# Moving the pool with x and its split parts above the weight buffers and temporaries in SBUF

## The chip, the core and the metric

The kernel runs on one core of a Trainium2 chip. The metric is the device time in microseconds (us) of one execution. A profile of one execution, with the duration and the start of each instruction on each engine, is read beside the times. The engines are PE (the matrix engine; PEld are its weight loads), DVE (vector), ACT (scalar), POOL and SP; SP issues nearly all transfers here.

## The reference

The program is an encoder trunk of two layers over 256 tokens of width 1024, all in float32. A layer is a mixer and a convolutional feed-forward:

```python
for l in range(DEPTH):
    h = _rmsnorm(x, mix_norm[l])
    x = x + _mixer(h, w_in[l], ...)      # gated delta rule + HGRN2, both directions
    h = _rmsnorm(x, ffn_norm[l])
    x = x + _conv_ffn(h, w_up[l], ...)   # 1024 -> 2 x 2816, conv of 3, SiLU gate, -> 1024
return _rmsnorm(x, final_norm)
```

Nearly all of the arithmetic is in the matrix products with w_in, the two branch weights, w_out, w_up and w_down.

## The kernel before, in words

Activations stay in SBUF with channels on the partitions and tokens in the free direction. A product is made with both operands split in two float32r parts, high and low: the weight piece `raw` (128 x 1024) is loaded by SP, ACT copies it to `wh` (line 204), and DVE writes the rest, `wl = raw - wh` (line 205). There are three buffers each of `raw`, `wh` and `wl`, used in turn. Each product then takes three matmuls per 128 x 128 block of weights (lines 240 to 242):

```python
self.g.mm(o, whm, a)      # high weights, high activations
self.g.mm(o, whm, b)      # high weights, low activations
self.g.mm(o, wlm, a)
```

Each such matmul (line 146) loads 128 columns of weights (512 bytes of each partition) into PE and streams 256 columns of activations (1024 bytes of each partition) past them. The next weights are loaded while the present activations stream. The names of the streamed operands tell the stages apart. In the trace a name in front of the comma is the streamed operand, the one behind it the loaded one:

- `xh`, `xl`: the split input of a mixer or of the feed-forward. They are streamed 3 x 1152 times. In 3 x 160 further matmuls, whose output has tokens on the partitions, they are the loaded operand and `wh`, `wl` are streamed. Of the 3 x 1152, 2 x 22 x 48 = 2112 belong to the product with w_up.
- `ohl`: the normalized outputs of the two mixer branches, for the branch weights (`pbr`, lines 928 to 930): 384 matmuls.
- `mhi`, `mlo`: the merged branches, for w_out: 3 x 128 matmuls.
- `hh`, `hl`: the hidden activations of the feed-forward, for w_down: 3 x 352 matmuls.

`xh`, `mhi` and `hh` go through the same helper (class `Gemm`, line 208), with the same order of instructions; only the tiles differ. A few products (lists in `OPT["f32"]`) are made in plain float32 from `raw` and `xnt`, which the trace shows as two matmuls each.

SBUF is given out by tile pools, one above the other in the order in which they are opened: `cp` holds constants, `xp` holds x, x times the norm's weight (`xw`), sums of squares and the split parts `xh` and `xl`, `wp` the weight buffers, `tp` temporaries. The pools of a stage, with `ohl`, `mhi`, `hh` and the rest (`mp0`, `fp0`, `mp1`, `fp1`), are opened above these and closed again. The order of the instructions is set by a scheduler from priorities in the code and does not look at addresses.

Of the kernel before, what the change touches and what calls it, by code (L numbers as in the profile page):

```python
# [14 lines left out]
PSUM = bass.MemoryType.PSUM  # L15
DRAM = bass.MemoryType.DRAM

P = 128
T = 256
# [55 lines left out]

# columns of the per-layer vector pack (one value per partition each)
V_MIX = 0
# [9 lines left out]

# columns of the constants
C_ID = 0
# [27 lines left out]
def trunk(ctx: ExitStack, tc: tile.TileContext, x_in, consts, masks, vec, rows, w16, w_in, w_br, w_out, w_up, w_down, out):  # L117
    nc = tc.nc
    PRE = OPT["pre"]
# [3 lines left out]
    cp = ctx.enter_context(tc.tile_pool(name="cp", bufs=1))  # L123
    xp = ctx.enter_context(tc.tile_pool(name="xp", bufs=1))
    wp = ctx.enter_context(tc.tile_pool(name="wp", bufs=3))
    tp = ctx.enter_context(tc.tile_pool(name="tp", bufs=4))
    pg = ctx.enter_context(tc.tile_pool(name="pg", bufs=3, space=PSUM))
    pm = ctx.enter_context(tc.tile_pool(name="pm", bufs=5, space=PSUM))
# [10 lines left out]
    class Group:  # L139
        """Matmuls accumulating in one PSUM bank, kept in order; one start, one stop."""  # L140

# [3 lines left out]
        def mm(self, o, lhsT, rhs, after=None):  # L145
            self.prev = chain(pe.matmul(o, lhsT, rhs, start=self.i == 0, stop=self.i == self.n - 1), self.prev)  # L146
            chain(self.prev, after)
            self.i += 1

    # ---------------------------------------------------------------- constants  # L150
    epst = cp.tile([P, 1], F32, name="epst")
# [3 lines left out]
    x = []  # L155
# [9 lines left out]
    for item in OPT["x0"]:  # L165
        if item < 4:
            sp.dma_start(xt[item], x_in[item])
        else:
            s = slice(512 * (item - 4), 512 * (item - 3))
# [9 lines left out]
    lower = cst[:, C_L:C_L + P]  # L179
    ones = cp.tile([P, P], F32, name="ones")  # L180
    pool.memset(ones, 1.0)

    # ---------------------------------------------------------------- helpers
    def tmp(name, tag="tmp"):
        return tp.tile([P, 512], F32, tag=tag, name=name, bufs=OPT[tag])

    def piece(src, n):
        raw = wp.tile([P, 1024], F32, tag="raw", name="raw", bufs=OPT["raw"])
        sp.dma_start(raw[:, :n], src)
        return raw  # L190
# [17 lines left out]
    class Gemm:  # L208
        """src[i]: [P, k, 256] pieces; fills a bank: two column tiles (T layout) or two token tiles."""

# [38 lines left out]
    def gemm32(src, xw, tokens=False):  # L249
        """As gemm, with float32 operands as they are."""  # L250
        ps = pg.tile([P, 512], F32, tag="g", name="ps", bufs=OPT["g"])
        g = Group(KT * 2)
        for k0 in range(0, KT, 4):
            raw = piece(src(k0 // 4), 1024).rearrange("p (k c) -> p k c", c=256)
            for kk in range(4):
                a = xw[k0 + kk]
                for m in range(2):
                    o = ps[:, m * 256:(m + 1) * 256]
                    if tokens:
                        g.mm(o, a[:, m * P:(m + 1) * P], raw[:, kk, :])  # L260
                    else:
                        g.mm(o, raw[:, kk, m * P:(m + 1) * P], a)
        return ps
# [6 lines left out]
    class Rms:  # L270
        """1 / sqrt(mean of squares + eps) of the tokens: on all partitions (rb), and per token (rt)."""

# [38 lines left out]
    class SplitX:  # L311
        """x times the norm's weight, in two parts."""

# [15 lines left out]
    class Pre:  # L329
        """The first projections of a mixer (PRE), from x times the norm's weight."""  # L330

# [12 lines left out]
        def ahead(self, l):  # L344
            """Splits the weights of some more projections."""
            if not OPT["es"][l]:
                return
            self.stack = ExitStack()
            pool = self.stack.enter_context(tc.tile_pool(name=f"ep{l}", bufs=1, side="right", reuse_waits=OPT["rw"]))
            n = 2 * len(OPT["es"][l])  # L350
            with tc.high_priority(offset=OPT["eo"]):
                for c in OPT["es"][l]:
                    self.parts[c] = [split_piece_(w_in[l, c, i], 1024, pool, n) for i in range(2)]
# [5 lines left out]
        def mm(self, items, after=None):  # L359
            """Products of (projection, k), one after the other."""  # L360
            for j, k in items:
                w = self.raw[j][k // 4].rearrange("p (k c) -> p k c", c=256)
                for m in range(2):
                    self.g[j].mm(self.ps[j][:, m * 256:(m + 1) * 256], w[:, k % 4, m * P:(m + 1) * P], self.x[k],
                                 after or self.last)
                    after = None
                    self.last = self.g[j].prev
# [4 lines left out]
    def mixer(l, pre, rs):  # L372
        V = vecs[:, l]
        with ExitStack() as mc:
# [11 lines left out]
            def small(name, n=8):  # L386
                return mp.tile([P, 2, n], F32, name=name)
# [14 lines left out]

            # ---- 1 / rms; the first projections are scaled after the product, the others before
            xw = pre.x
# [8 lines left out]
            rbp, rt = rs  # L413
            rb = mp.tile([P, T], F32, name="rb")
# [16 lines left out]

            # ---- beta, decays and their sums, tokens on partitions
            beta, cs, nea = small("beta"), small("cs"), small("nea")
# [48 lines left out]

            # ---- projections, conv and silu of q, k, v: [channel, token]
            qk = mp.tile([P, 2, H, T], F32, tag="qk", name="qk")
# [32 lines left out]

            # ---- sums of squares of q and k; k and v with tokens on partitions
            ssk = mp.tile([P, 2, H], F32, name="ssk")
# [49 lines left out]

            # ---- decays: exp of the smaller difference serves both directions  # L570
            dfb = []
# [20 lines left out]

            # ---- Gram blocks: per direction and block the transposed system [0] and the attention weights [1]
            np_ = mp.tile([P, 2, 2, 8, P], F32, tag="np", name="np_")
# [9 lines left out]

            # ---- inverses of the diagonal 32 x 32 blocks, one system per partition, columns on two halves
            def solve():
# [40 lines left out]

            # ---- T: inverse, R: its transpose. Blocks of 32 to 64 to 128
            def inverse():
# [41 lines left out]

            # ---- delta rule: first chunk, state, second chunk, outputs
            osb = []
# [50 lines left out]

            # ---- gates
            sgs, sz = [], []
# [21 lines left out]

            # ---- HGRN2, two heads at a time
            hg = {}  # L770
# [32 lines left out]
            def hgrn(e):  # L803
                qr, kb, t0 = hg["q", e], hg["k", e], hg["f", e]
                qa = late().tile([P, 2, 512], F32, tag="qa", name="qa")
                t1 = late().tile([P, 2, 256], F32, tag="tt1", name="tt1")
                at = late().tile([P, 2, 2, T], F32, tag="at", name="at")
                # qa: [backward, forward]; kb, t0: [forward, backward]
                dve.tensor_tensor(qa[:, 0], qr, t0[:, 1], ALU.mult)
                dve.tensor_tensor(qa[:, 1], qr, t0[:, 0], ALU.mult)  # L810
                ks = tmp("ksum", "tmh")
                dve.tensor_tensor(ks, kb[:, 0], kb[:, 1], ALU.add)
                # the block pairs u = (head, block): diagonal blocks of the weights, [s, t]
                diag = view(at[:, 0, 0, 0:1], [[512, 2], [384, 2], [1, P]])
                offd = view(at[:, 0, 0, P:P + 1], [[512, 2], [128, 2], [1, P]])
                pa = bank("pa", (2, 2, P), "h")
                for u in range(4):
                    pe.matmul(pa[:, u // 2, u % 2], ks[:, u * P:(u + 1) * P], qr[:, u * P:(u + 1) * P],
                              start=True, stop=True)
                act.copy(diag, pa)  # L820
                tc_, tn = t0, t1
                for n, h in enumerate(LEVELS):
# [6 lines left out]
                    for u in range(4):  # L829
                        pe.matmul(pa[:, u // 2, u % 2], kc[:, u * P:(u + 1) * P],  # L830
                                  view(qa[:, 0, u * P:u * P + 1], [[2 * h, 64 // h], [512 + h, 2], [1, h]]),
                                  start=True, stop=True)
# [34 lines left out]
                ob = late().tile([P, 2, 2, P], F32, tag="ob", name="ob", bufs=OPT["obb"])  # L867
# [5 lines left out]
            def out_norm(kind, ob, b, h0, nh, cc, sz, w):  # L873
                """ob: [P tokens, nh, 128] of block b, normalized, gated, transposed and split."""
                if not hl:
# [15 lines left out]
                for h in range(nh):  # L891
                    on = tp.tile([P, P], F32, tag=("s128", "s12h")[kind], name="on", bufs=(5, 2)[kind])
# [16 lines left out]

            # ---- branches, merge, output projection  # L910
            mh, ml = [], []
# [130 lines left out]
    def meet(pre, rs, todo, n):  # L1042
        """The rest of the first projections, the sums of squares among them."""
        pre.mm(todo[:n])
        rm, rs = rs, rs.finish(pre.last if n else None)
        pre.mm(todo[n:], rm.last)
        return rs, rm

    first = [raw0]
# [9 lines left out]
    rs, rm = meet(pre, rs, todo[OPT["e0"]:], OPT["fa0"])  # L1059
    # lower bounds of the forget gates: softmax over the layers, cumulated, less the first  # L1060
    lbm = cp.tile([P, 8], F32, name="lbm")
# [29 lines left out]
    for l in range(OPT["layers"]):  # L1091
        nxt = mixer(l, pre, rs)
        pre, rs = ffn(l, *nxt)
    # ---- final norm: tokens on partitions
    op = ctx.enter_context(tc.tile_pool(name="op", bufs=4, reuse_waits="tile"))
# [11 lines left out]
    rt = rs.per_token(prev)  # L1107
    prev = rs.last
    turn(3)
    for i in range(4):  # L1110
        h, b = divmod(i, 2)
        o = op.tile([P, 4 * P], F32, tag="o", name="o")
        src = pts[i].rearrange("p k c -> p (k c)")
# [84 lines left out]
```

## Time and profile before

| What | Value |
|---|---|
| time, median of three runs | 928.67 us (927.70 to 929.71) |
| span of the profiled execution, first to last instruction | 926.8 us |
| PE busy | 906.6 us, 98% |
| DVE busy | 668.5 us, 72% |
| ACT busy | 559.0 us, 60% |
| split float32r matmuls on PE | 3456 + 480 with x, 384 with ohl, 384 with mhi and mlo, 1056 with hh and hl |

The profile gives the profiled execution's own time as its span alone; the median lies 1.9 us above it, which is what lies around the span. Matmuls are pipelined: the duration of one (285 ns, say) is longer than the distance from its start to the next start, and only that distance, the pitch here, adds up to time. It is read where the chain of work that ended last is an unbroken run of matmuls: the length of the run divided by their number.

### The profile page before, as it was taken

The page shows a single profiled execution, that of the slowest core. Times are in us where ns is not written, and L with a number is a line of the kernel's source. Part 1 is how long each engine was busy: PE and PEld are TensorE (multiplying, and loading weights), DVE is VectorE, ACT ScalarE, POOL GpSimd, SP SyncE. Part 2 cuts the span into 40 slices and gives each one's busy share as a digit, 9 for nine tenths or more (in the row PEclk, how much of TensorE's full clock was granted, in tenths as well). Part 3 has the DMA queues.
Part 4 walks back from the last instruction along what each step waited for, and adds up shares of the span by engine and source line. Part 5 has one row for each costly group of instructions (what it writes and reads, how often), then busy time and mean ns, then how long its engine had stood idle before and what let it go on. Part 6 is the DMA issues. An engine that isn't in the chain of part 4 may idle for free.

```text
span 926.8 us, 18732 instructions
## 1 busy us (share of the span) xinstructions
PE 906.6 (98%) x7450; PEld 887.8 (96%) x7450; DVE 668.5 (72%) x1279; ACT 559.0 (60%) x974; POOL 13.9 (2%) x123
## 2 busy tenths in 40 slices
PE   7999999999999999999999999999999999999997
PEld 6988999999999999999989899999999999999996
DVE  4667997655877888865447889885667788888543
ACT  4698647678566555543437856665855665555443
POOL 0000000000000000000000000000000000000000
PEclk9999999999999999999999999999999999999999
DMA  6455554225567655555505564533265656555552
GB/s 207 137 189 169 171 184 124 69 74 177 183 202 250 186 183 183 183 176 174 171 27 170 183 205 149 152 100 92 91 197 175 192 184 187 183 183 183 171 183 80
DMA packets 51111, 150.07 MB, mean 162 GB/s; under 512 B 13488, under 2 KB 14032, under 8 KB 50768
## 3 DMA queue, kind: packets, MB, share of 16 engines
q1 hardware_dynamic: 50304, 147.96, 50.5%
q8 instruction: 58, 0.95, 0.4%
q10 hardware_dynamic: 720, 0.92, 0.3%
q14 instruction: 29, 0.24, 0.1%
HBM read 146.75 MB, written 2.11 MB: 161 GB/s over the span
## 4 chain that ended last, share of the span: by engine, by line
PE 88%; ACT 4%; DMA 3%; DVE 3%; issue 1%; SPq 0%; DVEq 0%; ACTq 0%
PE ps L146 72%; PE pbr L146 5%; PE pa L830 3%; DMA raw<-in_w_in_dram 2%; DVE wl L205 1%; DMA ld<-dg 1%; PE po L146 1%; PE poh L146 1%; PE psb L146 1%; ACT wh L204 1%; PE ss L146 0%; PE pz L666 0%; PE pr L689 0%; DMA xs<-in_consts_dram 0%; DVE pr L627 0%
## 5 line engine op out<-in xcount | busy, mean ns | idle before, releaser
L204 ACT CAST wh<-raw 128x1024 fp32r<-128x1024 f32 x244 | 251.8, 1035 | 250.7 <-PE ps L146 96.0
L205 DVE TENSOR_TENSOR wl<-raw,wh 128x1024 fp32r<-128x1024 f32 x244 | 293.6, 1205 | 127.1 <-ACT wh L204 123.7
L146 PE MATMUL ps<-xh,wl 128*128 128x256 f32 x1152 | 327.2, 285 | 1.5 <-DVE wl L205 1.5
L146 PE MATMUL ps<-xh,wh 128*128 128x256 f32 x1152 | 327.1, 285 | 1.2 <-ACT wh L204 1.2
L146 PE MATMUL ps<-xl,wh 128*128 128x256 f32 x1152 | 326.2, 284 | 0.0
L146 PEld LDWEIGHTS ps<-xh,wl 128*128 128x128 f32 x1152 | 220.1, 192 | 2.3 <-DVE wl L205 2.1
L146 PEld LDWEIGHTS ps<-xh,wh 128*128 128x128 f32 x1152 | 220.3, 192 | 1.7 <-ACT wh L204 1.4
L146 PEld LDWEIGHTS ps<-xl,wh 128*128 128x128 f32 x1152 | 220.3, 192 | 0.1
L146 PE MATMUL ps<-hl,wh 128*128 128x256 f32 x352 | 99.0, 281 | 0.0
L146 PE MATMUL ps<-hh,wl 128*128 128x256 f32 x352 | 99.0, 281 | 0.0
L146 PE MATMUL ps<-hh,wh 128*128 128x256 f32 x352 | 98.6, 280 | 0.0
L146 PEld LDWEIGHTS ps<-hh,wl 128*128 128x128 f32 x352 | 66.3, 188 | 0.1
L146 PEld LDWEIGHTS ps<-hl,wh 128*128 128x128 f32 x352 | 66.3, 188 | 0.1
L146 PEld LDWEIGHTS ps<-hh,wh 128*128 128x128 f32 x352 | 66.3, 188 | 0.0
L146 PE MATMUL ps<-xnt,raw 128*128 128x256 f32 x256 | 58.8, 380 | 0.0
L146 PEld LDWEIGHTS ps<-xnt,raw 128*128 128x128 f32 x256 | 47.0, 190 | 6.0
L146 PE MATMUL ps<-wl,xh 128*128 128x256 f32 x160 | 47.1, 294 | 0.7 <-DVE wl L205 0.6
L146 PE MATMUL ps<-wh,xh 128*128 128x256 f32 x160 | 46.6, 292 | 0.2 <-ACT wh L204 0.2
L146 PE MATMUL ps<-wh,xl 128*128 128x256 f32 x160 | 46.1, 288 | 0.0
L1001 DVE SCALAR_TENSOR_TENSOR cv<-fpad,vecs,cv 128x256 f32<-128x256 f32 x88 | 42.2, 480 | 4.3
L146 PE MATMUL pbr<-ohl,wh 128*128 128x256 f32 x256 | 45.3, 280 | 0.0
L146 PEld LDWEIGHTS pbr<-ohl,wh 128*128 128x128 f32 x256 | 38.8, 188 | 0.0
(274 smaller groups left out, 1438.1 us busy)
## 6 DMA issues: line engine op xcount, KB each, us to landing
raw<-in_w_in_dram SPq DMA_DIRECT2D x99, 512.0 KB, 3.6
raw<-in_w_up_dram SPq DMA_DIRECT2D x88, 512.0 KB, 3.7
raw<-in_w_down_dram SPq DMA_DIRECT2D x40, 512.0 KB, 3.6
raw<-in_w_br_dram SPq DMA_DIRECT2D x16, 512.0 KB, 3.9
raw<-in_w_out_dram SPq DMA_DIRECT2D x16, 512.0 KB, 4.2
cb<-cd SPq DMA_DIRECT2D x2, 1024.0 KB, 5.6
early<-in_w_in_dram SPq DMA_DIRECT2D x4, 512.0 KB, 7.2
raw<-in_w_down_dram SPq DMA_DIRECT2D x8, 256.0 KB, 3.3
```

Source lines behind the costliest of these rows:

```text
L146: self.prev = chain(pe.matmul(o, lhsT, rhs, start=self.i == 0, stop=self.i == self.n - 1), self.prev)
L204: act.copy(wh[:, :n], raw[:, :n])
L205: dve.tensor_tensor(wl[:, :n], raw[:, :n], wh.bitcast(F32)[:, :n], ALU.subtract)
L830: pe.matmul(pa[:, u // 2, u % 2], kc[:, u * P:(u + 1) * P], view(qa[:, 0, u * P:u * P + 1], [[2 * h, 64 // h], [512 + h, 2], [1, h]]), sta ...
L1001: dve.scalar_tensor_tensor(cv, pad[:, i:i + T], w[:, i:i + 1], cv, op0=ALU.mult, op1=ALU.add)
```

## The change

The pool `xp` is opened after `wp` and `tp` instead of before them:

```diff
     cp = ctx.enter_context(tc.tile_pool(name="cp", bufs=1))
-    xp = ctx.enter_context(tc.tile_pool(name="xp", bufs=1))
     wp = ctx.enter_context(tc.tile_pool(name="wp", bufs=3))
     tp = ctx.enter_context(tc.tile_pool(name="tp", bufs=4))
+    xp = ctx.enter_context(tc.tile_pool(name="xp", bufs=1))
```

The other lines of the diff take comments out. On every engine the instructions, their order and their waits are the same in both programs; what differs is the address of the 1047 tiles that lie in these three pools. In bytes from the start of a partition, as the two programs are built:

| Tiles | before | after | moved by |
|---|---|---|---|
| x (four tiles) | 21536 to 29832 | 77408 to 85704 | +55872 |
| xw | 29856 | 85728 | +55872 |
| xh, xl, xh, xl | 40160, 44256, 48352, 52448 | 96032, 100128, 104224, 108320 | +55872 |
| raw (three) | 56544, 60640, 64736 | 21536, 25632, 29728 | -35008 |
| wh (three) | 68832, 72928, 77024 | 33824, 37920, 42016 | -35008 |
| wl (three) | 81120, 85216, 89312 | 46112, 50208, 54304 | -35008 |
| temporaries | 93408 to 112416 | 58400 to 77408 | -35008 |
| ohl, layer 0 and 1 | 112416, 159680 | the same | 0 |
| mhi, layer 0 and 1 | 139008, 155392 | the same | 0 |
| mlo, layer 0 and 1 | 130816, 147200 | the same | 0 |
| hh and hl, 44 tiles in steps of 1024 | from 125824 | the same | 0 |

## Rows read from the trace of the kernel before

**Rows 1.** The page's first two parts: busy time, share of the span and number of instructions of each engine, and DVE's busy tenths and PE's granted clock (in tenths) in 40 equal slices of the span.

```profile
PE 906.6 (98%) x7450; PEld 887.8 (96%) x7450; DVE 668.5 (72%) x1279; ACT 559.0 (60%) x974; POOL 13.9 (2%) x123
DVE  4667997655877888865447889885667788888543
PEclk9999999999999999999999999999999999999999
```

**Rows 2.** The page's chain of work that ended last, as shares of the span by engine.

```profile
PE 88%; ACT 4%; DMA 3%; DVE 3%; issue 1%; SPq 0%; DVEq 0%; ACTq 0%
```

**Rows 3.** Groups of instructions by line, engine and operation: out<-in, shapes, count, busy us, mean ns of one, idle time before them.

```profile
L146 PE MATMUL ps<-xh,wl 128*128 128x256 f32 x1152 | 327.2, 285 | 1.5 <-DVE wl L205 1.5
L146 PE MATMUL ps<-hh,wl 128*128 128x256 f32 x352 | 99.0, 281 | 0.0
L146 PE MATMUL ps<-wl,xh 128*128 128x256 f32 x160 | 47.1, 294 | 0.7 <-DVE wl L205 0.6
L146 PE MATMUL pbr<-ohl,wh 128*128 128x256 f32 x256 | 45.3, 280 | 0.0
L146 PE MATMUL pbr<-ohl,wl 128*128 128x256 f32 x128 | 34.4, 280 | 0.0
L146 PE MATMUL ps<-mhi,wl 128*128 128x256 f32 x128 | 35.5, 279 | 0.0
```

**Rows 4.** The chain of work that ended last, asked for ten windows: start us, length us, engine, output and line, number of instructions. In order: x with w_up in layer 0 and in layer 1; x in the mixer of layer 0; merged branches (mhi, mlo) with w_out in layer 0 and in layer 1; ohl with the branch weights in layer 0 and in layer 1; hidden activations (hh, hl) with w_down in layer 0, in the first half of layer 1 and in the second half of layer 1.

```profile
289.94 100.08 PE ps L146 x834
...
744.90 100.20 PE ps L146 x835
...
211.42 8.40 PE ps L146 x70
...
251.95 21.12 PE ps L146 x181
...
704.88 21.12 PE ps L146 x181
...
235.00 15.08 PE pbr L146 x128
...
687.97 15.15 PE pbr L146 x128
...
404.95 10.09 PE ps L146 x86
...
856.93 28.16 PE ps L146 x240
...
887.91 14.12 PE ps L146 x119
```

**Rows 5.** Windows of 10 us in which PE never pauses: busy time and number of instructions of PE, PEld, DVE, ACT and POOL, granted clock, share of the DMA engines, GB/s. In order: two of x with w_up; one of mhi and mlo; two of hh and hl.

```profile
290.00:300.00 10.00, 10.00 (x86) 10.00 (x85) 9.57 (x18) 7.84 (x13) 0.27 (x4) 1.00 0.63 200
...
800.00:810.00 10.00, 10.00 (x85) 10.00 (x85) 7.99 (x15) 5.88 (x10) 0.27 (x4) 1.00 0.58 176
...
710.00:720.00 10.00, 10.00 (x88) 10.00 (x87) 7.03 (x11) 6.87 (x10) 0.00 (x0) 1.00 0.57 166
...
890.00:900.00 10.00, 10.00 (x87) 10.00 (x86) 4.35 (x4) 2.72 (x3) 0.00 (x0) 1.00 0.57 178
905.00:915.00 10.00, 10.00 (x86) 10.00 (x86) 3.14 (x3) 4.10 (x5) 0.00 (x0) 1.00 0.15 45
```

**Rows 6.** The timeline of PE in layer 0 with w_up: start us, duration us, instruction. Over these instructions the address of the loaded weights steps by multiples of 512 bytes, that of the streamed operand by multiples of 1024 bytes.

```profile
300.10 0.28 PE L146 MATMUL ps<-xl,wh 128*128 128x256 f32 x1
300.22 0.28 PE L146 MATMUL ps<-xh,wl 128*128 128x256 f32 x1
300.34 0.28 PE L146 MATMUL ps<-xh,wh 128*128 128x256 f32 x1
300.46 0.28 PE L146 MATMUL ps<-xl,wh 128*128 128x256 f32 x1
300.58 0.28 PE L146 MATMUL ps<-xh,wl 128*128 128x256 f32 x1
```

**Rows 7.** Groups of DVE and ACT that read or write the moved tiles, columns as in rows 3.

```profile
L205 DVE TENSOR_TENSOR wl<-raw,wh 128x1024 fp32r<-128x1024 f32 x236 | 288.0, 1222 | 117.5 <-ACT wh L204 114.1 <-PE ps L146 2.4
L204 ACT CAST wh<-raw 128x1024 fp32r<-128x1024 f32 x236 | 246.8, 1049 | 235.5 <-issue 91.5 <-PE ps L146 83.7 <-DMA raw<-in_w_in_dram 21.6
L267 DVE TENSOR_TENSOR xl<-xnt,xh 128x1024 fp32r<-128x1024 f32 x4 | 4.8, 1217 | 0.0
L425 DVE TENSOR_TENSOR xnt<-xw,rbc 128x1024 f32<-128x1024 f32 x4 | 4.7, 1216 | 1.3 <-ACT rb L415 1.3
L266 ACT CAST xh<-xnt 128x1024 fp32r<-128x1024 f32 x4 | 4.2, 1046 | 2.8 <-DVE xnt L425 2.6
```

**Rows 8.** Windows over whole stages, columns as in rows 5: the mixer of layer 0; from its w_out to the end of the feed-forward; the mixer of layer 1; from its w_out to the last w_down.

```profile
25.00:251.00 226.00, 222.18 (x1851) 215.29 (x1851) 166.77 (x376) 161.27 (x305) 3.30 (x10) 1.00 0.47 147
251.00:470.00 219.00, 219.00 (x1819) 218.19 (x1818) 154.07 (x245) 114.73 (x167) 2.80 (x44) 1.00 0.58 187
480.00:704.00 224.00, 222.17 (x1853) 215.59 (x1852) 175.95 (x382) 148.56 (x299) 3.49 (x14) 1.00 0.47 145
704.00:921.00 217.00, 215.99 (x1814) 215.46 (x1812) 153.67 (x241) 118.55 (x177) 2.80 (x44) 1.00 0.55 172
```

## The prediction

> **What bounds the kernel now.** I read the page from the top: busy shares first, then the chain of waits, then the chain and the engines' windows stage by stage. [...] The chain that ended last lies on PE for 88% [rows 2], and from w_out to the end of the feed-forward PE never pauses in layer 0 and for 1 us of 217 in layer 1 [rows 8]. So the time is mostly a count of matmuls times their pitch, start to start. That pitch cannot be had from the mean durations of 279 to 294 ns, which overlap [rows 3]; it comes from the unbroken runs of the chain [rows 4]:
>
> x 100.08/834 = 120.0 ns in layer 0, 100.20/835 = 120.0 in layer 1 and 8.40/70 = 120.0 in the mixer; mhi and mlo 21.12/181 = 116.7 in both layers; ohl 15.08/128 = 117.8 and 15.15/128 = 118.4; hh and hl 10.09/86 = 117.3, 28.16/240 = 117.3 and 14.12/119 = 118.7.
>
> All of these are the same instruction: 128 columns of weights loaded, 256 columns streamed, float32r. x and mhi even pass through the same helper. What differs between them is where the streamed operand lies. The company of the other engines does not sort them: hh runs at 118.7 with the DMA engines 57% busy and with 15% [rows 4, 5]; x stands at 120.0 with the vector engine at 9.6 or at 8.0 of 10 us, mhi at 116.7 with 7.0 [rows 5]. So I take the pitch to depend on addresses, and addresses are all that the change touches.
>
> **Which part of the address.** In x the starts follow each other by exactly 0.12 us while the weights' address steps by multiples of 512 bytes and the operand's by multiples of 1024 [rows 6]. So only the part below 512 bytes seems to count. The load of the next weights runs beside the present stream, so a natural measure is the distance of the streamed operand from the weights, modulo 512, from the table of addresses: x 0, mhi 32, ohl of layer 0 64, hh 160, ohl of layer 1 224. In that order the pitches are 120.0, 116.7, 117.8, 117.3 or 118.7, 118.4: the highest at distance 0, the lowest just beyond it. After the change the distances are x 256, mhi 224, ohl 256 and 416, hh 352. Alternatively the operand's own start counts: x comes to 96032, which is 16384 bytes below ohl of layer 0, so both have the same start modulo any of these sizes.
>
> **The change part by part.** No instruction, wait or transfer is added, removed or reordered, so no queue is passed and no wait is new.
>
> Matmuls that stream x, or load it with the weights streamed: 3 x 1152 + 3 x 160 = 3936 [rows 3]. 2112 of them (w_up) lie wholly on the path. The other 1824 are in the mixers. PE's part of the chain is 0.88 x 926.8 = 816 us; the two stretches in which PE is busy throughout take 219 and 217 us of it [rows 2, 8], which leaves 380 of the remaining 491 us, 77%. So 2112 + 0.77 x 1824 = 3516 matmuls count. Their new pitch has no row. From below it is bounded by 116.7, the lowest pitch of any placement; from above by 123.3, as far above 120.0 as the lowest is below it. I take 118.1, the mean of ohl's two rows, whose own start (layer 0) x will share: 3516 x -1.9 ns = -6.7 us. The bounds give -11.6 and +11.6 us.
>
> Matmuls that stream ohl, mhi, hh: 384, 384 and 1056. Their tiles stay, but the weights beneath them move, so by the distance they are dealt anew. I take the mean of the six different pitches (120.0, 116.7, 117.8, 118.4, 117.3, 118.7), 118.15. mhi: 384 x +1.45 = +0.6 us. hh, now at about 117.8 over its three rows: 1056 x +0.35 = +0.4 us. ohl, now at 118.1: 0. Together +1.0 us; the bounds, all at 116.7 or all at 120.0, are -1.7 and +4.3 us.
>
> Vector and scalar engine: raw, wh and wl move together, so their distances to each other stay. Three placements of a split cost 1222, 1217 and 1216 ns on the vector engine, two cost 1049 and 1046 ns on ACT [rows 7]. Six ns on 236 splits are 1.4 us either way on an engine with 28% to spare: nothing on the path, 1.4 us if that cover were gone. In the densest window the vector engine has 9.57 of 10 us of work [rows 5]; PE faster by 1.6% would ask for 9.7, which still fits. Transfers keep size and order, and the DMA engines are at most 63% busy in these windows [rows 5]: nothing, either way.
>
> Sum against the profiled execution: 926.8 - 6.7 + 1.0 = 921.1 us of span, and 1.9 us around it as in the median of the runs: 923 us, 0.6% faster than 928.67.
>
> [...]
>
> **The rivals.**
>
> *Placement has no part in it.* The pitches differ for a cause that I don't see, and the new addresses leave them. For it: hh has two pitches, 117.3 and 118.7, at the same addresses [rows 4], so something besides the address has a hand in it. Against it: x returns to 120.0 in both layers and in the mixer. Time: 928.7. This is also the case in which moving the pools does nothing at all.
>
> *Only the part below 256 bytes counts* (slower). The distance of x is then 0 before and after, and x stays at 120.0. The others move: ohl of layer 0 from 64 to 0, x's old place: 192 x +2.2 = +0.4 us. mhi from 32 to 224, the old place of ohl of layer 1: 384 x +1.7 = +0.7 us. ohl of layer 1 goes from 224 to 160, hh's old place: 0. hh goes from 160 to 96, which no row shows: 1056 matmuls at 117.3 to 120.0, -0.5 to +2.3 us. So 929.2 to 932.1, and 931 in the middle. It decides from the point where hh comes to 118.6 (1.1 + 0.8 us is 0.2%). For it: five placements fit a period of 256 as well as one of 512. Against it: nothing yet.
>
> *x gets worse than 120.0*: no row shows such a pitch; at the bound it is +11.6 + 1.0 us, 941. Against it: x holds the highest of all pitches now, and the rest lie within 2 ns of each other.
>
> **How the numbers follow.** About 0.2% (1.9 us) is what a measurement of this kernel can tell from no change. The forecast has a chance of 0.47, placement without a part 0.20, the period of 256 bytes 0.25, x above 120.0 0.08. Faster by over 0.2%: nearly all of the forecast, 0.45. Slower: 0.15 of the period of 256 (hh at 118.6 or more) and all of the last, 0.23. Within 0.2%: the rest, 0.32. The forecast's own range is x between 116.7 and 118.7, -11.6 to -4.6 us with +1.0 for the others, 918 to 925. With the other cases the range is 917 to 932.5: from x at its lowest bound to the upper end of the second rival.
>
> **What would show it.** In the chain of the changed kernel a window of 100 us of w_up holds some 847 matmuls in place of 834 if x comes to 118.1; 834 again is the second rival or the first, and mhi's and ohl's runs then tell these two apart (118.4 and 120.0 against 116.7 and 117.8). If the distance counts, or the own start with the same weights, x and ohl of layer 0 now have the same pitch. The forecast is wrong if x's pitch stays or rises, or if the time moves while all pitches stay.

## The result and the profile after

The changed kernel took 933.39 us (median of four runs, 931.57 to 935.81) against 928.28 us before: a ratio of 1.0053, 95% interval 1.0035 to 1.0071. It is slower. 923 us was forecast, and the measured time lies above the range of 917 to 932.5.

The profiled execution of the changed kernel has a span of 934.0 us against 926.8. The numbers of instructions are the same on every engine, and the vector engine and ACT are as busy as before [rows 1]; PE is busy 6.4 us longer. From the page of the changed kernel (busy time and share of the span; below it chosen groups with count, busy us, mean ns and idle time before them, which answer to [rows 3] and [rows 7]):

```profile
PE 913.0 (98%) x7450; PEld 893.6 (96%) x7450; DVE 669.1 (72%) x1279; ACT 559.1 (60%) x974; POOL 13.9 (1%) x123
...
L204 ACT CAST wh<-raw 128x1024 fp32r<-128x1024 f32 x244 | 251.9, 1035 | 258.8 <-PE ps L146 115.0
L205 DVE TENSOR_TENSOR wl<-raw,wh 128x1024 fp32r<-128x1024 f32 x244 | 293.6, 1205 | 132.9 <-ACT wh L204 129.5
L146 PE MATMUL ps<-xh,wl 128*128 128x256 f32 x1152 | 327.5, 286 | 1.5 <-DVE wl L205 1.5
...
L146 PE MATMUL ps<-hh,wl 128*128 128x256 f32 x352 | 99.9, 284 | 0.0
```

The page of the kernel before has, for the same two groups of ACT and DVE:

```profile
L204 ACT CAST wh<-raw 128x1024 fp32r<-128x1024 f32 x244 | 251.8, 1035 | 250.7 <-PE ps L146 96.0
L205 DVE TENSOR_TENSOR wl<-raw,wh 128x1024 fp32r<-128x1024 f32 x244 | 293.6, 1205 | 127.1 <-ACT wh L204 123.7
```

These groups also hold eight splits of half the width, which [rows 7] leave out; so their means lie below the 1049 and 1222 ns there. x at 286 ns is where it was (285 before); hh went from 281 to 284 ns. As before, the pitch comes from the chain of work that ended last, asked for windows inside unbroken runs (start us, length us, what, number of matmuls). In order: x with w_up; mhi and mlo with w_out in layer 0; ohl in layer 0 and in layer 1; hh and hl in layer 0 and in layer 1:

```profile
290.97 100.08 PE ps L146 x834
...
253.14 20.94 PE ps L146 x177
...
236.00 14.04 PE pbr L146 x117
...
693.96 14.08 PE pbr L146 x120
...
403.89 30.12 PE ps L146 x251
...
861.96 28.08 PE ps L146 x234
```

Divide length by number and compare with [rows 4]. The distances are those of the second rival, streamed operand minus weights modulo 256 bytes.

| Streamed | before: distance, pitch | after: distance, pitch | matmuls | change |
|---|---|---|---|---|
| x | 0, 120.0 ns | 0, 120.0 ns | 3936 | 0 |
| hh, hl | 160, 117.3 or 118.7 | 96, 120.0 | 1056 | +2.3 us |
| mhi, mlo | 32, 116.7 | 224, 118.3 | 384 | +0.6 us |
| ohl, layer 0 | 64, 117.8 | 0, 120.0 | 192 | +0.4 us |
| ohl, layer 1 | 224, 118.4 | 160, 117.3 | 192 | -0.2 us |

For hh before I take 117.8: in its trace five of the eight w_down products run at 117.3 and three at 118.7. The sum is +3.1 us, where the medians differ by 5.1 (four runs each; the larger set of e7 gives 3.6) and the two spans by 7.2. A further piece of the span is PE's clock. Windows of the changed kernel (busy time and number of instructions of PE, PEld, DVE, ACT, POOL; granted clock; DMA share; GB/s):

```profile
475.00:484.00 9.00, 9.00 (x51) 8.13 (x51) 3.86 (x5) 2.59 (x4) 0.20 (x4) 1.00 0.01 2
484.00:492.00 8.00, 8.00 (x31) 6.97 (x31) 7.02 (x18) 7.72 (x14) 0.13 (x2) 0.57 0.00 0
492.00:500.00 8.00, 8.00 (x39) 7.04 (x38) 4.06 (x19) 1.10 (x2) 0.13 (x2) 1.00 0.44 131
```

Between 484 and 492 us the granted clock averages 0.57 of full speed; from 485 to 490 us it is 0.50. Some 10 us before, PE had waited 1.0 us for the norm, and then it ran plain float32 and small matmuls, as it does in the kernel before, whose granted clock is 1.00 in this place:

```profile
485.00:490.00 5.00, 5.00 (x25) 4.41 (x24) 4.27 (x14) 4.93 (x8) 0.13 (x2) 1.00 0.14 16
490.00:495.00 5.00, 5.00 (x25) 4.41 (x24) 3.61 (x18) 0.81 (x3) 0.13 (x2) 1.00 0.58 193
```

What the drop costs is seen in the chain there: the 32 small matmuls (psb) and the float32 projections behind them. The changed kernel:

```profile
482.45 4.38 PE psb L146 x32
486.83 9.45 PE ps L146 x32
```

and the kernel before:

```profile
480.28 3.48 PE psb L146 x32
483.76 13.91 PE ps L146 x64
```

4.38 - 3.48 = 0.9 us, and 9.45 against half of 13.91, 2.5 us: 3.4 us. So the 7.2 us between the two spans are 3.1 us of pitches, 3.4 us of clock, and 0.7 us whose cause is open. By the starts of the same instructions in both traces, these arise in the two mixers ahead of ohl, less than 0.5 us in each.

### The profile page after: what moved, and what is told of

Same layout as the page of the kernel before. It is cut to its first block, busy times and chain, and to the rows that moved or that the text cites. A ratio compares the mean times of both kernels' runs of the same rounds, so it can differ in the third digit from the quotient of the medians.

```text
span 934.0 us, 18732 instructions
## 1 busy us (share of the span) xinstructions
PE 913.0 (98%) x7450; PEld 893.6 (96%) x7450; DVE 669.1 (72%) x1279; ACT 559.1 (60%) x974; POOL 13.9 (1%) x123
## 2 busy tenths in 40 slices
DMA packets 51111, 150.07 MB, mean 161 GB/s; under 512 B 13488, under 2 KB 14032, under 8 KB 50768
## 4 chain that ended last, share of the span: by engine, by line
PE 85%; DVE 5%; ACT 5%; DMA 4%; issue 1%; SPq 0%; DVEq 0%; ACTq 0%
PE ps L146 69%; PE pbr L146 5%; PE pa L830 3%; DMA raw<-in_w_in_dram 2%; DVE wl L205 2%; PE psb L146 1%; PE po L146 1%; PE poh L146 1%; ACT wh L204 1%; DVE cacc L507 1%; ACT e L581 0%; DMA ld<-dg 0%; PE ss L146 0%; ACT cacc L500 0%; PE pz L666 0%
## 5 line engine op out<-in xcount | busy, mean ns | idle before, releaser
L204 ACT CAST wh<-raw 128x1024 fp32r<-128x1024 f32 x244 | 251.9, 1035 | 258.8 <-PE ps L146 115.0
L205 DVE TENSOR_TENSOR wl<-raw,wh 128x1024 fp32r<-128x1024 f32 x244 | 293.6, 1205 | 132.9 <-ACT wh L204 129.5
L146 PE MATMUL ps<-xnt,raw 128*128 128x256 f32 x256 | 61.3, 392 | 0.0
```

Source lines behind the costliest of these rows:

```text
L204: act.copy(wh[:, :n], raw[:, :n])
L205: dve.tensor_tensor(wl[:, :n], raw[:, :n], wh.bitcast(F32)[:, :n], ALU.subtract)
```

## The experiments

All but e7 put unused bytes in front of chosen pools. No instruction and no wait changes, only addresses. The theory after the result was that the pitch of these matmuls is set by the distance of the streamed operand from the weights, modulo 256 bytes; the rivals were the own start of an operand, the distance modulo 512, and causes other than placement. In the diffs a number of float32 columns times 4 is the padding in bytes.

**e1: the changed kernel with the distances of before.** 64 bytes in front of the mixers' and the feed-forwards' pools.

```diff
-            hp = []
+            mp.tile([P, 16], F32, name="padm"); hp = []
...
-            hh, hl = [], []
+            fp.tile([P, 16], F32, name="padf"); hh, hl = [], []
```

> The changed kernel with 64 bytes of padding at the start of the mixers' and the feed-forwards' pools, so that all distances of streamed operands from the weights are, modulo 256 bytes, those of the kernel before (x 0, mhi 32, ohl 64 and 224, hh 160); modulo 512 they differ from before by 256, and x and the weights stay at the changed kernel's addresses. Theory (the distance modulo 256 sets the pitch): all five pitches come back, x 120.0, mhi 116.7, ohl 117.8 and 118.4, hh 117.3 or 118.7, and the time is that of the kernel before, 928. Rival (the own start of an operand, or the distance modulo 512): no reason for the five to come back together; the time stays near 933.

Measured: 928.77 us, ratio to before 0.9998 (0.9986 to 1.0010). The chain in windows of mhi, of ohl in layer 0 and in layer 1, of hh in layer 1:

```profile
250.96 21.12 PE ps L146 x181
...
233.89 14.13 PE pbr L146 x120
...
687.48 13.61 PE pbr L146 x115
...
857.97 26.05 PE ps L146 x222
```

That is 116.7, 117.8, 118.3 and 117.3 ns: all back together, with x still above the weights. The whole loss is undone by 64 bytes of padding per pool, so the order of the pools as such costs nothing. Modulo 512 the distances were not those of before, so that rival falls.

**e2: only x's distance.** The kernel before with 224 bytes in front of the weight buffers, which takes x from distance 0 to 32.

```diff
-    raw0 = wp.tile([P, 1024], F32, tag="raw", name="raw", bufs=OPT["raw"])
+    wp.tile([P, 56], F32, tag="padw", name="padw", bufs=1); raw0 = wp.tile([P, 1024], F32, tag="raw", name="raw", bufs=OPT["raw"])
```

> The kernel before with 224 bytes of padding in front of the weight buffers: everything above x moves up together, so that only x's distance changes, from 0 to 32 modulo 256 (the distance of mhi in the kernel before). Theory: x goes from 120.0 to 116.7 and, in the 480 matmuls where x is loaded and the weights are streamed (distance 224), to 118.3; all other pitches stay. (2112 + 0.77 x 1344) x -3.3 - 0.77 x 480 x 1.7 ns = -11 us, so 917. Rival (own start): x's tiles have not moved, x stays at 120.0 and the time at 928; what moved are the others, with unknown sign.

Measured: 919.17 us, ratio 0.9892 (0.9873 to 0.9911), a gain of 9.6 us where 11 was expected; 917 lies at the lower edge of its five runs (917.07 to 921.74). x with w_up and hh in layer 0:

```profile
289.95 100.10 PE ps L146 x858
...
397.99 26.05 PE ps L146 x222
```

858 matmuls in 100 us where [rows 4] have 834: 116.7 ns, the pitch that mhi has at this distance. x's own tiles have not moved by a byte. hh stays at 117.3 in the window shown. The own start of the streamed operand is refuted here as the cause for x.

**e3: everything moves, no distance does.** The kernel before with 64 bytes at the bottom of SBUF.

```diff
-    epst = cp.tile([P, 1], F32, name="epst")
+    cp.tile([P, 16], F32, name="padc"); epst = cp.tile([P, 1], F32, name="epst")
```

> The kernel before with 64 bytes of padding at the very bottom: every tile moves up by 64 bytes, no distance changes; the weights and x start at 32 modulo 256 as in the changed kernel. Theory: no pitch changes, 928. Rival (own start of weights or of the streamed operand): pitches change, the more so as weights and x have the starts modulo 256 of the changed kernel; 930 or more.

Measured: 929.49 us, ratio 1.0006 (0.9996 to 1.0017). x, mhi, ohl of layer 0 and hh at the end of layer 1:

```profile
289.99 100.08 PE ps L146 x834
...
251.89 21.12 PE ps L146 x181
...
234.93 14.13 PE pbr L146 x120
...
886.97 14.12 PE ps L146 x119
```

120.0, 116.7, 117.8 and 118.7: as before. That both starts moved by 64 bytes did not count; that their difference changed did (e2, x from 120.0 to 116.7 ns).

**e4: the two distances that no run had shown.** As e2 with 128 bytes in front of the weights (x at 128), and 32 bytes in front of the feed-forwards' pool (hh at 192).

```diff
+    wp.tile([P, 32], F32, tag="padw", name="padw", bufs=1); ...
+            fp.tile([P, 8], F32, name="padf"); ...
```

> The kernel before with 128 bytes in front of the weight buffers and 32 bytes at the start of the feed-forwards' pool: x's distance is 128 (also where x is loaded), hh's 192, neither of which any run shows yet. Theory: mhi and ohl keep 116.7, 117.8 and 118.4; x and hh show two new values, each between 116.7 and 120.0, so the time lies between 916 and 930. Rival (own start): x's tiles have not moved and it stays at 120.0.

A single run: 928.65 us, with the lowest mean granted clock of all runs (0.991), so that this time says nothing. The pitches do. In order: x with w_up; x in the mixer; hh in layer 0; hh in the second half of layer 1.

```profile
289.96 100.16 PE ps L146 x844
...
120.58 4.44 PE ps L146 x37
...
436.90 15.19 PE ps L146 x129
...
887.97 14.07 PE ps L146 x124
```

x at 128 runs at 118.7 in one stretch and at 120.0 in another; hh at 192 at 117.8 and at 113.5. I had expected one value for each distance, none below 116.7. There are two at each of these distances, and one of the four lies below 116.7.

**e5: x at 192.** As e2 with 64 bytes.

```diff
+    wp.tile([P, 16], F32, tag="padw", name="padw", bufs=1); ...
```

> The kernel before with 64 bytes in front of the weight buffers: only x's distance changes, from 0 to 192 modulo 256 (where x is loaded, to 64). In the run of e4 hh at distance 192 ran at 113.5 ns in some stretches and at 117.8 in others. Theory: x does the same, each stretch at one of the two; (2112 + 0.77 x 1344) matmuls x -6.5 or -2.2 ns and 0.77 x 480 x -2.2 ns (117.8, the pitch at 64) give -8 to -21 us, 908 to 921. Rival (what e4 showed at 192 belongs to hh, not to the distance): x stays between 116.7 and 120.0 with one pitch, 917 or more.

Measured: 920.36 us, ratio 0.9902 (0.9887 to 0.9917). That is inside 908 to 921, but also inside the rival's 917 or more, so the pitches have to decide. x with w_up, x in the mixer of layer 0, and mhi in layer 0:

```profile
289.98 100.11 PE ps L146 x850
...
210.29 7.74 PE ps L146 x68
...
250.40 20.64 PE ps L146 x172
```

The long stretch is at 117.8, the one in the mixer at 113.8: two pitches, one of them far below 116.7, as hh had in e4, so the rival falls. And mhi, whose distance of 32 was not touched, is at 120.0 in this layer, where the kernel before, e1, e2 and e3 have 116.7. So this distance also has a second pitch.

**e6 and e7: the loss in its parts.** e7 is the changed kernel in more runs; e6 is the changed kernel with 64 bytes in front of the feed-forwards' pool only (the second half of e1's diff), so that hh alone goes back.

> The changed kernel with 64 bytes at the start of the feed-forwards' pool alone: hh's distance goes back from 96 to 160, all else stays as changed. Theory: hh goes back from 120.0 to 117.3 or 118.7, mhi stays at 118.3, ohl at 120.0 and 117.3; 1056 x (117.7 - 120.0) ns = -2.4 us against the changed kernel run beside it: the largest part of the loss. Rival (the loss is mostly something else than pitches, such as clock drops that the change brings): the time stays at that of the changed kernel, less than 1 us off.

> The changed kernel as it is, in more runs. The pitches read from its first profile (hh 120.0, mhi 118.3, ohl 120.0 and 117.3) add up to 1056 x 2.3 + 384 x 1.65 + 192 x 2.2 - 192 x 1.0 ns = +3.3 us; its first profiled execution also had PE's clock at half for 6.8 us, which the kernel before did not. Theory (pitches are the whole of it, the clock drop is chance): the median comes to 931.5 to 932.5. Rival (the change also makes the clock drop): it stays at 933.4 or more, and a profile shows the drop at the same place again.

Measured beside each other: changed 933.30 us, ratio to before 1.0038 (1.0025 to 1.0051); with hh back 930.44 us, 1.0005 (0.9996 to 1.0015). hh of e7 in layer 0, then of e6 in layer 0:

```profile
403.93 30.12 PE ps L146 x251
```

```profile
403.98 26.05 PE ps L146 x222
```

120.0 back to 117.3 ns, and 2.9 us of the loss of 3.6 gone, where 2.4 was expected. So hh is the largest part, as the table has it. The median of e7 lies above the 931.5 to 932.5 that I expected, but so does that of before in this set (929.69): the difference, 3.6 us, fits the 3.1 of the pitches. By its absolute time, 933.30, the run lies between the two conditions, and the rival's second sign, a drop of the clock, came true: in e7's profiled run it came again, shorter (0.81 on average over 9 us, which is 3.4 us if it was at 0.50 as in the first profile):

```profile
475.00:484.00 9.00, 8.48 (x32) 7.22 (x33) 2.64 (x3) 2.87 (x4) 0.00 (x0) 0.81 0.01 2
484.00:492.00 8.00, 8.00 (x54) 7.49 (x53) 7.02 (x15) 5.75 (x11) 0.20 (x4) 1.00 0.00 0
```

It is not the change's own: e4, which is the kernel before with padding, has it too (0.83 from 468 to 478 us, 0.76 from 478 to 492). The mean granted clock of the profiled run is 0.996, 0.994 and 0.996 in e2, e5 and e6, beside 0.995 in e7, and 0.997, 0.998 and 0.997 in e1, e3 and e8; and among 23 runs of the kernel before the mean granted clock lies between 0.994 (931.8 us) and 0.999. Nor does it make the difference: the mean granted clock of e7's six runs is 0.9962 on average, that of the 17 runs of before beside them 0.9965, and 0.0003 of 932 us is 0.3 us of the 3.6. What sets a drop off was not tried.

**e8: x and hh at 192.** As e5, with 32 bytes in front of the feed-forwards' pool.

```diff
+    wp.tile([P, 16], F32, tag="padw", name="padw", bufs=1); ...
+            fp.tile([P, 8], F32, name="padf"); ...
```

> As e5, and 32 bytes at the start of the feed-forwards' pool, so that hh is at distance 192 too (before 160). Theory: hh runs at 113.5 or 117.8 per stretch, against 117.7 on the mean now: 0 to -4.4 us more than e5. Rival as for e5: no more than 1 us either way.

Measured: 918.96 us, ratio 0.9885 (0.9871 to 0.9899), 1.4 us below e5. x in the mixer, x with w_up, hh in the first half of layer 1 and in the third quarter, and mhi in layer 0:

```profile
209.11 7.96 PE ps L146 x70
...
289.99 100.11 PE ps L146 x850
...
845.89 26.15 PE ps L146 x222
...
875.90 14.19 PE ps L146 x125
...
248.99 21.12 PE ps L146 x176
```

113.7, 117.8, 117.8, 113.5 and again 120.0 ns. hh thus has both pitches that it had in e4. The 1.4 us are within the spread of e5's runs (918.07 to 922.54), so this time does not decide between theory and rival. This is the fastest version of all, 1.2% below the kernel before, though not told apart from e2 by its interval. Were the w_up stretches at the 113.5 of that hh stretch, near the 113.7 of x in the mixer, they would give another 2112 x 4.3 ns = 9 us (an estimate from these rows); what sets a stretch on the one or the other was not tried.

## Why the prediction was wrong, point by point

- *PE bounds the time, and its pitch depends on addresses alone.* Right in the main. e2 moved one distance and the time by 1.1%, e3 moved every address and nothing else, and the time stayed (ratio 1.0006). "Alone" is too much: at the same addresses hh has 117.3 and 118.7 [rows 4].
- *"So only the part below 512 bytes seems to count."* Right as a bound, and it failed in the use I made of it. [rows 6] exclude the parts from 512 up; they don't say whether the bit of 256 counts. I took it to count, which makes x's move from 0 to 256 a new place. With the period of 256 that e1 shows, x goes from 0 to 0. This is the step that failed: the term 3516 x -1.9 ns = -6.7 us is 0; x stayed at 120.0. With it at 0 and the others at the measured +3.1, the prediction's own sum gives 926.8 + 3.1 + 1.9 = 931.8 us.
- *The own start as the alternative.* Wrong by e2 and e3. That x and ohl of layer 0 would have the same pitch came true (120.0 both), but because their distances are the same, not their starts.
- *The others dealt anew: +1.0 us, at most +4.3.* Measured from the pitches: +3.1 us. The miss is hh, put at +0.4 us and measured at +2.3: its new place had no row, and the mean of six pitches was no guide to it. That mhi's +0.6 came out is luck, since 118.15 happens to lie near the 118.3 of its new place. The second rival's look-up by place was the better guide: it said +0.4 for ohl of layer 0 (+0.4), +0.7 for mhi (+0.6), 0 for ohl of layer 1 (-0.2), -0.5 to +2.3 for hh (+2.3).
- *Vector engine, ACT and transfers: nothing.* Right for the two engines: 1205 and 1035 ns on the pages of both kernels; the bytes moved are the same, 150.07 MB. (One of the three "placements of a split", the 1216 ns [rows 7], is no split but the multiplication that makes xnt; nothing hangs on it.)
- *The second rival* had 929.2 to 932.1 us and a chance of 0.25, of which 0.15 slower. It was the case. Its upper end of 932.1 still lies below both medians of the changed kernel. In the first set (933.39) the 5.1 us are more than the pitches give, and the clock does not explain it (0.997 on average in its four runs, as in the 23 runs of the kernel before beside e1); that remainder stays open. In the second set (933.30) the kernel before stands 1 us higher too, and the difference is 3.6 us, of which 3.1 are pitches. I set its chance too low: the same five rows fitted both periods, as the prediction says itself, and 256 needs only that fewer bits count.

## What to carry to other kernels

Where PE is the bound with float32r matmuls that load new weights each time, the difference of the two operands' addresses modulo 256 bytes is a tuning knob worth trying; in this kernel it gave 1.1% (e2, 919.17 us against 928.74). Pad a pool by 32 bytes at a time and read the pitch from unbroken runs of the chain. In this kernel it was by these differences that a change of layout was to be judged, not by where a pool lies: with all of them as before, the moved pools took 928.77 us (e1). If the same rows fit two periods, both cases are to be priced as equals before one of them is made the forecast.

## What the runs showed of the hardware

Pitch of a float32r matmul of 256 streamed columns with 128 loaded, by the distance of the streamed operand from the weights modulo 256 bytes, over the kernel before, the changed one and the eight experiments:

| 0 | 32 | 64 | 96 | 128 | 160 | 192 | 224 |
|---|---|---|---|---|---|---|---|
| 120.0 | 116.7; mhi of layer 0 in e5 and e8 120.0 | 117.8 | 120.0 | 118.7 or 120.0 | 117.3 or 118.7 | 113.5 or 117.8 | 118.3 |

So the distance does not give the pitch; in these stretches a distance has one pitch or two. I had not expected that (113.5 and 117.8 ns at 192, say). A pitch was kept over hundreds of matmuls: x with w_up stays at 120.0 ns through 834 in layer 0 of the kernel before. It changed where a few other matmuls broke in, without PE falling idle: in layer 1 of the kernel before, three small matmuls at 885.9 us stand between hh at 117.3 and hh at 118.7, and PE is busy for all of the 2 us from 885 to 887. What makes the choice is open. That the difference of the addresses counts is measured (x from 120.0 to 116.7 ns in e2, none of the four pitches read in e3 changed); what causes it, the runs don't show. All weight buffers lie alike modulo 256, so the runs can't tell either whether the weights in use or the next ones, just being loaded, count. Distances between the multiples of 32 bytes were not tried.
